# Moving a runtime branch and a small projection ahead of the last product of a mixture of experts

## The chip, the cores and the metric

The kernel runs on one core of one Trainium2 chip. The time is device microseconds of one execution; lower is better. In the profile, PE is TensorE's matmul stream, PEld its weight loads, DVE VectorE, ACT ScalarE, POOL GpSimd and SP SyncE, which issues every DMA of this kernel. A small q behind an engine's name (SPq, PEldq) means its instruction queue: branches, register loads, semaphore instructions and DMA issues.

## The reference, cut to what matters

Two layers of a decoder trunk over 256 tokens of width 1024, all float32. Each layer has a token mixer, a norm, a channel mixer, a second norm, and a per-layer embedding. The channel mixer of layer 0 is dense; the one of layer 1 is the mixture of experts that the change is about. Only the end of layer 1 is touched:

```python
def moe_swiglu(x, w_router, w1, w3, w2):      # x: 256 x 1024, 8 experts, d_ff 3584
    top_logits, top_e = lax.top_k(x @ w_router, 2)
    gates = softmax(top_logits)
    # for each expert e, over the tokens that chose it:
    y = (silu(x_e @ w1[e]) * (x_e @ w3[e])) @ w2[e]
    # each token adds its two experts' y, each times its gate

h = layer_norm(ALPHA * h + moe_swiglu(h, ...), g, b)
h = h + sigmoid(h @ ple_gate) * (p @ ple_proj)   # p: 256 x 256
```

## The kernel before, in words

**Words and buffers.** Weights ("words") come in loads of mostly 1 MB through one function, `load_raw` (line 79). It takes the next buffer of a cycle over the rings that are open at that point: raw (4 buffers of 1 MB), side (3), post (3) and early (2), in the mixture twelve in all. SP issues the loads in the order of the program, and each waits for its buffer to be free. `split_unit` (line 94) splits words into a high part (ACT, line 103) and a low part (DVE, line 111); `mm3` (lines 142 to 144) multiplies with three matmuls.

**The mixture** (`swiglu_moe`, line 987). Experts are ranked by how many tokens chose them. Ranks 0 to 4 have room for 128 tokens (class `Big`, split words), rank 5 for 64 and ranks 6 and 7 for 32 (class `Small`, words used unsplit, 128/n row groups of the array side by side). `STEPS` is the order, written out by hand: 26 pairs (rank, column block). Each step runs in `experts_in` (line 1312): the up product with w1, SiLU, the down product of the step before, the up product with w3, `sl` = `sl` times gate times that product (line 1367), and, after an expert's last block, `put_back`. `gather` (line 1096) makes a one-hot matrix `oh` from token slots, multiplies the tokens out with it, transposes them, and also transposes `oh` itself into `ohT` (line 1138) and takes each row's gate as `gs` (lines 1140 and 1144). `put_back` (lines 1202 and 1288) splits the down product, multiplies by `ohT`, and `add_back` (line 1303) adds into `h` with a running row sum for the norm. The last step is (6, 1): rank 6, the second block of 1536 of its 3584 columns, whose down product needs six loads of 1 MB.

**The end.** After step (6, 1): its `turn` (line 1253, PE transposes and an ACT copy), its down product (line 1283), then `closing` (line 1412), which is called ahead of the put-back: it loads p, transposes it (line 280), loads and splits the words of ple_proj and the first 1 MB of ple_gate (the latter's low part on POOL), and loads the two rows of the norm (line 347). Then the put-back. Then a flag is read into a register on every engine (`values_load`, line 1385) and `tc.If` (line 1386) branches past a further round of all experts, which is needed only where an expert got more tokens than it has places; for these inputs it is skipped. A block of `If` is scheduled as a unit: nothing behind it runs ahead of it. Its round takes words through the raw ring alone, since `closing` has taken the others out. Then, outside, `norm_turn` (line 403) runs with `ple_project` (line 326, 24 matmuls over 4 banks, then 4 ACT copies) between its parts on PE, and `ple` (line 433) with 96 matmuls of the gate, sigmoid, product, sum, and the output's DMAs.

```python
                before_[0].down(gT, before_[1])
                rest = closing() if base == 0 else None
                finish_last()
...
            flag = nc.values_load(over[0:1, 0:1], min_val=0, max_val=1)
            with tc.If(flag > 0):
                experts(1)
```

Of the kernel before, what the change touches and what calls it, by code (L numbers as in the profile page):

```python
# [28 lines left out]
PLE = 256  # L29
# [24 lines left out]
def body(ctx, tc, nc, I, out):  # L54
# [115 lines left out]
    slots = consts.tile([128, 256], FT, name="slots")  # L170
# [12 lines left out]
    def fill_constants(words):  # L183
        left = [0]

        def scratch(shape, dt):
# [3 lines left out]
            if len(shape) == 2:  # L190
# [16 lines left out]
        nc.gpsimd.iota(slots, pattern=[[1, 256]], base=1, channel_multiplier=0,  # L207
                       allow_small_or_imprecise_dtypes=True)
        nc.vector.memset(halfpi, PI / 2)
# [193 lines left out]
    def norm_turn(hT, produce, gb, sm, z, sq, each=None, meanwhile=None):  # L403
# [3 lines left out]
        if produce is None:  # L407
            bring = meanwhile()
# [8 lines left out]
        if produce is not None:  # L417
            bring = meanwhile and meanwhile()
# [568 lines left out]
    def swiglu_moe(hT, logits, closing):  # L987
        hh, hl = hT
        with tc.tile_pool(name="moe", bufs=1, reuse_waits="tile") as mp:
# [11 lines left out]
            lg2 = mp.tile([128, NT, 2, N_EXP], FT, name="lg2")  # L1001
            nc.vector.tensor_copy(lg2, ps)
            lg = mp.tile([128, NT, N_EXP], FT, name="lg")
# [9 lines left out]
            ohe = mp.tile([128, NT, 2, N_EXP], FT, name="ohe")  # L1013
# [20 lines left out]
            xg_h = pers.tile([128, KD, 256], FR, name="xgh", tag="hTh")  # L1034
            xg_l = pers.tile([128, KD, 256], FR, name="xgl", tag="hTl")
# [19 lines left out]
            def ranks():  # L1055
# [12 lines left out]
                words = mp.tile([128, 1024], FT, name="words", tag="sl")  # L1068
# [27 lines left out]
            def gather(r, n, off, half):  # L1096


                small = n < 128
                sr, gr = (slot, gate) if r == 0 else (slot_r, gate_r)  # L1100
                oh = mp.tile([128, NT, 128], FR, name="oh", tag="oh", bufs=1)
                for t in range(NT):
                    done["oh"] = nc.vector.tensor_scalar(
                        oh[:, t].rearrange("p (j s) -> p j s", s=n),
                        slots[:, None, off:off + n].to_broadcast([128, 128 // n, n]),
                        sr[:, t, r:r + 1], None, op0=OP.is_equal)
# [5 lines left out]
                for f in range(2):  # L1112
                    fs = slice(f * 512, (f + 1) * 512)
                    p = work()
                    for t in range(NT):
                        nc.tensor.matmul(p, oh[:, t], hsh[:, t, fs], start=t == 0, stop=False)
                        nc.tensor.matmul(p, oh[:, t], hsl[:, t, fs], start=False, stop=t == NT - 1)
                    nc.scalar.activation(xs[:, fs], p, AF.Copy)
                if small:
                    x = mp.tile([128, KD, 64], FT, name="xe", tag="xe", bufs=1)[:, :, :n]  # L1120
                    p = work()[:, :KD * n].rearrange("p (a b) -> p a b", b=n)
                    for k in range(KD):
                        nc.tensor.transpose(p[:, k], xs[:n, k * 128:(k + 1) * 128], ident[:n, :n])
                    nc.scalar.activation(x, p, AF.Copy)
                else:
                    b0 = half * 128
                    x = xg_h[:, :, b0:b0 + 128], xg_l[:, :, b0:b0 + 128]
                    for k0 in range(0, KD, 4):
                        p = work().rearrange("p (a b) -> p a b", a=4)
                        for j in range(4):  # L1130
                            nc.tensor.transpose(p[:, j], xs[:, (k0 + j) * 128:(k0 + j + 1) * 128], ident)
                        ins = split_sb(x[0][:, k0:k0 + 4], x[1][:, k0:k0 + 4], p)
                    if off == 0 and r == 0:
                        table("silu_and_others", ins)
# [12 lines left out]
            class Big:  # L1147
# [4 lines left out]
                def __init__(self, r, got):  # L1152
                    self.r, (self.x, self.ohT, self.gs) = r, got
                    self.y = None

# [38 lines left out]
                def y_split(self, w, ys):  # L1194
                    yh = mp.tile([128, D], FR, name="yh", tag="gh")
                    yl = mp.tile([128, D], FR, name="yl", tag="gl")
                    for f, y in enumerate(ys):
                        fs = slice(f * w, (f + 1) * w)
                        split_sb(yh[:, fs], yl[:, fs], y)
                    return yh, yl  # L1200

                def put_back(self):
                    yh, yl = self.y_split(512, self.y)
                    for f in range(2):
                        fs = slice(f * 512, (f + 1) * 512)
                        for t in range(NT):
                            p = work()
                            nc.tensor.matmul(p, self.ohT[:, t], yh[:, fs], start=True, stop=False)
# [3 lines left out]
            class Small(Big):  # L1212
# [44 lines left out]
                def down(self, gT, c):  # L1257
                    if self.y is None:
                        self.y = acc()[:, :D // self.q]
# [219 lines left out]
```

## Time and profile before

| | us |
|---|---|
| median of 3 runs | 1515.63 (1511.83 to 1517.67) |
| the profiled execution | 1511.99 |
| its span, first to last instruction | 1510.2 |
| PE busy, share of the span | 1421.4, 94% |
| DVE busy | 975.8, 65% |
| ACT busy | 812.8, 54% |

The profile numbers everything in microseconds from the start of the span. A busy share counts overlapping work of an engine once, so PE at 94% says that PE is hardly ever empty, not that it is at its peak. The DMA share is the mean over the core's 16 DMA engines. Idle time of an engine costs something only where a later stage waits for it, so each stretch has to be asked which resource it waits for last. The mixture runs from about 598 to 1471 us; what is behind it is the norm, the projection and the gate.

### The profile page before, as it was taken

What the parts mean: (1) busy time and instruction counts of PE and PEld (TensorE: products, weight loads), DVE (VectorE), ACT (ScalarE), POOL (GpSimd) and SP (SyncE); (2) the same over time, 40 slices, a digit from 0 to 9 for tenths busy, and PEclk for the clock granted to TensorE, in tenths of its full rate; (3) what the DMA queues carried; (4) which work ended last, traced back from release to release, by engine and by line L of the source; (5) the groups of instructions that cost most, each with busy time, mean ns of one, the idle gap of its engine ahead of it and who ended that gap; (6) DMA issues with size and microseconds to landing.
All of it is one profiled execution on the core that took longest, in us unless ns stands there. A gap on an engine that the chain in (4) does not pass through costs nothing. (4 is left out here: it accounts for less than half of the span.)

```text
span 1510.2 us, 19841 instructions
## 1 busy us (share of the span) xinstructions
PE 1421.4 (94%) x7298; PEld 1054.7 (70%) x7298; DVE 975.8 (65%) x1347; ACT 812.8 (54%) x1120; POOL 8.1 (1%) x16
## 2 busy tenths in 40 slices
PE   7999899999999997988999989999899997999968
PEld 6677788888786776746877668853478755777736
DVE  7676654554676767626888568930288854898745
ACT  5466543443555466526766457720277644777534
POOL 0000000000000000000000000000000000000000
PEclk9999999999999998999999999999999999999989
DMA  8643655454346642999999999999999999999893
GB/s 282 221 153 133 223 185 205 167 192 171 99 150 206 224 154 75 383 419 412 406 413 344 408 405 413 416 382 398 414 407 413 405 408 412 407 413 403 304 362 112
DMA packets 125065, 456.84 MB, mean 303 GB/s; under 512 B 10976, under 2 KB 22048, under 8 KB 103200
## 3 DMA queue, kind: packets, MB, share of 16 engines
q1 hardware_dynamic: 124960, 455.50, 78.2%
q8 instruction: 59, 0.97, 0.3%
q14 instruction: 46, 0.38, 0.1%
HBM read 454.42 MB, written 1.05 MB: 302 GB/s over the span
## 5 line engine op out<-in xcount | busy, mean ns | idle before, releaser
L111 DVE TENSOR_TENSOR wlo<-raw,whi 128x1024 fp32r<-128x1024 f32 (+1 forms) x238 | 282.0, 1214 | 91.4 <-ACT whi L103 86.7
L103 ACT ACTIVATE whi<-raw 128x1024 fp32r<-128x1024 f32 (+1 forms) x238 | 243.1, 1052 | 119.9 <-PE acc L143 54.6
L142 PE MATMUL wk<-whi,xgh 128*128 128x512 f32 x560 | 224.0, 400 | 14.9 <-ACT whi L103 14.9
L143 PE MATMUL wk<-whi,xgl 128*128 128x512 f32 x560 | 221.4, 395 | 0.0
L111 DVE TENSOR_TENSOR wlo<-post,whi 128x1024 fp32r<-128x1024 f32 x132 | 157.6, 1219 | 74.2 <-ACT whi L103 72.4
L144 PE MATMUL wk<-wlo,xgh 128*128 128x512 f32 x560 | 201.8, 399 | 3.0 <-DVE wlo L111 3.0
L103 ACT ACTIVATE whi<-post 128x1024 fp32r<-128x1024 f32 x132 | 135.7, 1056 | 110.8 <-DMA post<-in_moe_w_dram 63.2
L111 DVE TENSOR_TENSOR wlo<-side,whi 128x1024 fp32r<-128x1024 f32 x136 | 162.2, 1218 | 15.5 <-ACT whi L103 9.9
L142 PE MATMUL acc<-whi,gh 128*128 128x512 f32 x392 | 155.1, 396 | 8.9 <-ACT whi L103 7.9
L143 PE MATMUL acc<-whi,gl 128*128 128x512 f32 x392 | 154.3, 394 | 0.0
L103 ACT ACTIVATE whi<-side 128x1024 fp32r<-128x1024 f32 x136 | 139.8, 1056 | 25.7 <-PE acc L143 14.2
L144 PE MATMUL acc<-wlo,gh 128*128 128x512 f32 x392 | 142.8, 395 | 0.5
L142 PEld LDWEIGHTS wk<-whi,xgh 128*128 128x128 f32 x560 | 106.9, 191 | 43.6 <-ACT whi L103 19.9
L144 PEld LDWEIGHTS wk<-wlo,xgh 128*128 128x128 f32 x560 | 105.2, 191 | 29.3 <-DVE wlo L111 7.2
L143 PEld LDWEIGHTS wk<-whi,xgl 128*128 128x128 f32 x560 | 106.9, 191 | 22.3 <-DVE xgl L138 0.2
L1367 DVE SCALAR_TENSOR_TENSOR sl<-sl,gs,wk 128x512 f32<-128x512 f32 (+2 forms) x43 | 30.2, 732 | 140.7 <-PE wk L1240 94.0
L142 PEld LDWEIGHTS acc<-whi,gh 128*128 128x128 f32 x392 | 73.5, 188 | 31.5 <-ACT whi L103 12.8
L142 PE MATMUL wk<-whi,hTh 128*128 128x512 f32 x224 | 88.7, 396 | 2.7 <-ACT whi L103 2.7
L144 PE MATMUL wk<-wlo,hTh 128*128 128x512 f32 x224 | 87.9, 393 | 0.0
L143 PE MATMUL wk<-whi,hTl 128*128 128x512 f32 x224 | 87.8, 392 | 0.0
L144 PEld LDWEIGHTS acc<-wlo,gh 128*128 128x128 f32 x392 | 72.7, 188 | 20.9 <-DVE wlo L111 4.4
L143 PEld LDWEIGHTS acc<-whi,gl 128*128 128x128 f32 x392 | 73.6, 188 | 16.6
(396 smaller groups left out, 2119.4 us busy)
## 6 DMA issues: line engine op xcount, KB each, us to landing
raw<-in_moe_w_dram SPq DMA_DIRECT2D x96, 1024.0 KB, 15.2
side<-in_moe_w_dram SPq DMA_DIRECT2D x75, 1024.0 KB, 15.1
post<-in_moe_w_dram SPq DMA_DIRECT2D x75, 1024.0 KB, 15.6
early<-in_moe_w_dram SPq DMA_DIRECT2D x50, 1024.0 KB, 15.8
raw<-in_ffn_w_dram SPq DMA_DIRECT2D x19, 1024.0 KB, 5.2
raw<-in_w_in_dram SPq DMA_DIRECT2D x15, 1024.0 KB, 7.3
post<-in_ffn_w_dram SPq DMA_DIRECT2D x14, 1024.0 KB, 5.2
raw<-in_moe_w_dram SPq DMA_DIRECT2D x17, 768.0 KB, 6.6
```

What stands on the lines that cost most here:

```text
L103: nc.scalar.activation(hi, v, AF.Copy)
L111: engine.tensor_sub(lo, v, hi.bitcast(FT))
L142: nc.tensor.matmul(ps, xh, wh, start=first, stop=False)
L143: nc.tensor.matmul(ps, xl, wh, start=False, stop=False)
L144: return nc.tensor.matmul(ps, xh, wl, start=False, stop=last)
L1367: nc.vector.scalar_tensor_tensor(sl[:, fs], sl[:, fs], now.gs, p, op0=OP.mult, op1=OP.mult)
```

## The change

Five edits.

1. The down product and put-back of step (6, 1) leave `experts_in`, which now returns after the step's `turn`. Behind it come, in this order: the rings but raw are taken away, the branch, the rings are given back, p is loaded and turned and the projection is done and copied out, the down product, the loads of the norm's rows, the put-back.
2. The flag is read at the fourth step of the mixture, not at the branch.
3. Rank 6 is accumulated and put back one block at a time (`by_step`), so there is a put-back of (6, 0) in the middle of the mixture, in the step behind it.
4. `gather` no longer transposes `oh` and no longer takes gates; `put_back` makes `ohT` itself (`back_of`): a diagonal of the slots (DVE), a matmul with a matrix of -1 (PE), a comparison (DVE). The gate is applied by `add_back` instead of by the product with w3.
5. The put-back of a small expert takes the row groups innermost, four banks at once. The early split of the gate's first words (ACT, POOL) goes. Code for other sizes of small experts comes in, and is not used with the sizes here.

```diff
+            def back_of(r, off, w, blocks):
+                sr = slot if r == 0 else slot_r
+                dg = mp.tile([128, NT, 128], FT, name="dg", tag="oh", bufs=1)
+                p = work()[:, :256]
                 for t in range(NT):
...
+                    nc.vector.tensor_scalar(dg[:, t], ident, sr[:, t, r:r + 1], None, op0=OP.mult)
+                    nc.tensor.matmul(p[:, t * 128:(t + 1) * 128], negones, dg[:, t], start=t == 0, stop=t == NT - 1,
+                                     skip_group_check=True)
+                ohT = []
+                for j in range(blocks):
+                    ohT.append(mp.tile([128, NT, 128], FR, name="ohT", tag="ohT", bufs=3))
+                    nc.vector.tensor_scalar(ohT[j], p.rearrange("p (t b) -> p t b", t=NT), float(off + j * w),
+                                            numbers[:, 128 // w // 2:128 // w // 2 + 1], op0=OP.add, op1=OP.is_equal)
+                return ohT
...
-                p = work()
-                ohT = mp.tile([128, NT, 128], FR, name="ohT", tag="ohT", bufs=3)
-                for t in range(NT):
-                    nc.tensor.transpose(p[:, t * 128:(t + 1) * 128], oh[:, t].bitcast(FT), ident)
-                for t in range(NT):
-                    nc.tensor.matmul(p[:, 256:257], oh[:, t].bitcast(FT), gr[:, t, r:r + 1],
-                                     start=t == 0, stop=t == NT - 1)
-                nc.scalar.activation(ohT, p[:, :256].rearrange("p (t b) -> p t b", t=NT), AF.Copy)
-                gs = mp.tile([128, 1], FT, name="gs", tag="gs", bufs=3)
-                nc.vector.tensor_copy(gs, p[:, 256:257])
-                return x, ohT, gs
...
                 def put_back(self):
+                    ohT = back_of(self.r, self.off, self.n, self.m)
+                    yh, yl = self.y_split(512, self.y)
...
-            def add_back(t, f, w, p):
+            def add_back(r, t, f, w, p):
                 fs = slice(f * w, (f + 1) * w)
-                nc.vector.scalar_tensor_tensor(h[:, t, fs], h[:, t, fs], 1.0, p, op0=OP.mult, op1=OP.add,
+                nc.vector.scalar_tensor_tensor(h[:, t, fs], p, (gate if r == 0 else gate_r)[:, t, r:r + 1], h[:, t, fs],
+                                               op0=OP.mult, op1=OP.add,
                                                accum_out=(sums if w == 512 else quarters)[:, t, f:f + 1])
...
                 def finish_last():
                     ex, c = before_
-                    if c == len(ex.cols) - 1:
+                    if c == len(ex.cols) - 1 or (base == 0 and ex.r == seq[-1][0]):
                         ex.put_back()
 
                 for s, (r, c) in enumerate(seq):
                     now = made[r]
+                    if s == 3 and base == 0:
+                        flag.append(nc.values_load(over[0:1, 0:1], min_val=0, max_val=1))
+                    if base == 0 and r == seq[-1][0] and c == 0:
+                        now.by_step(c)
...
-                turn_last()
-                before_[0].down(gT, before_[1])
-                rest = closing() if base == 0 else None
-                finish_last()
-                if rest is not None:
-                    rest()
-
-            experts(0)
-
-            flag = nc.values_load(over[0:1, 0:1], min_val=0, max_val=1)
-            with tc.If(flag > 0):
+                if base:
+                    turn_last()
+                    before_[0].down(gT, before_[1])
+                    finish_last()
+                    return
+                ex, c = before_
+                n = ex.cols[c][1] // 128
+                gT = mp.tile([128, 4, 128], FT, name="gk", tag="xe", bufs=1)[:, :n // 4]
+                return ex, c, ex.turn(g, c, gT)
+
+            flag = []
+            ex, c, gT = experts(0)
+
+            own = closing[0]()
+            with tc.If(flag[0] > 0):
                 experts(1)
+            closing[1](own)
+            ex.by_step(c)
+            ex.down(gT, c)
+            closing[2]()
+            ex.put_back()
             return sums
...
+                def away():
+                    return {n: rings.pop(n) for n in ("early", "post", "side")}
+
+                def project(own):
+                    rings.update(own)
                     n = PLE // 128 * S
...
+                    words = chunk("side")
+                    parts = [words[:, j * n:(j + 1) * n].rearrange("p (k s) -> p k s", s=S).bitcast(FR)
+                             for j in range(2)]
+                    ple_turn(i, pool.tile([128, NT, PLE], FT, name="pt", tag="sg", bufs=1), *parts)
+                    kept["pp"] = chunk("early").rearrange("p (t d) -> p t d", t=NT)
+                    ple_project(ple_weights(i), *parts, kept["pp"])()
+                    del rings["early"]
+
+                def vectors():
+                    kept["gb"] = load_gb("ffn", i, halves(chunk("post")))
+
+                closing = away, project, vectors
```

## Rows read from the trace of the kernel before

**Rows 1.** The page, 40 slices of the span: GB/s that the DMA engines moved.

```profile
GB/s 282 221 153 133 223 185 205 167 192 171 99 150 206 224 154 75 383 419 412 406 413 344 408 405 413 416 382 398 414 407 413 405 408 412 407 413 403 304 362 112
```

**Rows 2.** A stretch of 10 us (columns: PE, PEld, DVE, ACT, POOL busy; PE's clock; DMA share; GB/s).

```profile
1400.00:1410.00 10.00, 9.45 (x44) 7.46 (x43) 5.83 (x6) 4.82 (x7) 0.00 (x0) 1.00 0.64 256
```

**Rows 3.** Timeline: last w3 load, a slab read, turn's copy, down product, last load before the branch.

```profile
1434.95 0.42 SPq L87 DMA_DIRECT2D side<-in_moe_w_dram  x1
...
1447.86 0.83 PE L1240 MATMUL wk<-side,xe 128*32 128x384 f32 x8
...
1452.66 0.49 ACT L1254 ACTIVATE ge<-wk 128x384 f32<-128x384 f32 x1 [7.88 <-PE wk L1253]
...
1458.04 0.79 SPq L347 DMA_DIRECT2D post<-in_ln_ffn_b_dram  x1
1458.61 1.07 PE L1283 MATMUL acc<-post,ge 128*32 128x256 f32 x16 [1.42 <-DMA post<-in_moe_w_dram]
...
1461.19 0.64 PE L1283 MATMUL acc<-early,ge 128*32 128x256 f32 x8 [0.66 <-DMA early<-in_moe_w_dram]
```

**Rows 4.** DMA issues, us to landing: that w3 load, that last load, gate words alone.

```profile
side<-in_moe_w_dram SPq DMA_DIRECT2D x1, 768.0 KB, 11.1
...
post<-in_ln_ffn_b_dram SPq DMA_DIRECT2D x1, 512.0 KB, 13.2
...
raw<-in_ple_gate_dram SPq DMA_DIRECT2D x3, 1024.0 KB, 5.1
```

**Rows 5.** Line 1386, the branch (columns: duration in ns min/median/max; first and last start).

```profile
L1386 SPq EVENT_SEMAPHORE  x8: 17/17/17, 1465.0 to 1471.3; - x8
...
L1386 PEldq COMPARE_BRANCH  x1: 5782/5782/5782, 1464.2 to 1464.2; - x1
...
L1386 DVEq COMPARE_BRANCH  x1: 72/72/72, 1469.7 to 1469.7; - x1
...
L1386 DVEq EVENT_SEMAPHORE  x1: 21/21/21, 1472.7 to 1472.7; - x1
```

**Rows 6.** Waits of SP's queue (us in total, times, longest): the first load behind the branch.

```profile
SPq L87 <- DVEq L1386: 1.3, 1, 1.3
```

**Rows 7.** Timeline of the put-back and the norm: split, first add, last matmul, sums, tile 0.

```profile
1461.96 0.38 ACT L137 ACTIVATE yh<-acc 128x256 fp32r<-128x256 f32 x1 [8.80 <-PE acc L1283]
...
1463.50 0.42 DVE L1305 SCALAR_TENSOR_TENSOR h<-h,wk 128x256 f32<-128x256 f32 x1
1463.85 0.08 DVE L1305 DVE_READ_ACCUMULATOR h<-h,wk 128x1 f32 x1
...
1464.09 0.27 PE L1297 MATMUL wk<-yl,ohT 32*128 32x256 f32 x1
...
1469.02 2.34 DVE L1301 TENSOR_TENSOR sums<-quarters 128x4 f32<-128x4 f32 x1
...
1472.77 0.21 DVE L386 TENSOR_SCALAR lnnm<-sums 128x1 f32<-128x1 f32 x1 [1.41 <-DVEq L1386]
...
1476.28 1.41 DVE L400 SCALAR_TENSOR_TENSOR h<-raw,lnrs,post 128x512 f32<-128x512 f32 x2
```

**Rows 8.** The chain that ended last (start, us, what): projection, turn, gate, sigmoid.

```profile
1472.82 0.76 PE acc L142
...
1476.14 0.43 PE acc L143
...
1481.17 1.75 PE wk L280 x16
1482.92 0.23 PE acc L142
...
1505.11 0.61 ACT sg L440
```

**Rows 9.** A stretch of 1 us within the projection (columns as in rows 2).

```profile
1477.00:1478.00 1.00, 1.00 (x3) 0.79 (x3) 0.96 (x4) 0.60 (x1) 0.00 (x0) 0.50 1.04 401
```

**Rows 10.** Timeline of rank 0's gather: the matmuls that take the gates.

```profile
598.41 0.50 PE L1140 MATMUL wk<-gate,oh 128*128 128x1 f32 x4
```

More of the change, by code (lines that the diff above doesn't have):

```diff
@@ L1094, in of_expert, with gather @@
                 return I[name][0, bass.ds(expert[r], 1)].rearrange("e k n -> (e k) n")
[L1096 to L1101, printed above, removed]
+            def back_of(r, off, w, blocks):
+                sr = slot if r == 0 else slot_r
+                dg = mp.tile([128, NT, 128], FT, name="dg", tag="oh", bufs=1)
+                p = work()[:, :256]
                 for t in range(NT):
[L1103 to L1106, printed above, removed]
+                    nc.vector.tensor_scalar(dg[:, t], ident, sr[:, t, r:r + 1], None, op0=OP.mult)
[7 more added lines that the diff above has]
+                return ohT
+            def gather(r, n, off, x):
+                sr = slot if r == 0 else slot_r
+                oh = mp.tile([128, NT, 128], FR, name="oh", tag="oh", bufs=1)[:, :, :n]
+                for t in range(NT):
+                    done["oh"] = nc.vector.tensor_scalar(oh[:, t], slots[:, :n], float(off), sr[:, t, r:r + 1],
+                                                         op0=OP.add, op1=OP.is_equal)
                 if off == 0 and r == 0:
@@ L1226, in rows, with pieces, block @@
+                def pieces(self, w):
+                    for j in range(self.m):
+                        o = 0
+                        while o < w:
+                            at = j * w + o
+                            n = min(512 - at % 512, w - o)
+                            yield j, o, at // 512, at % 512, n
+                            o += n
                 def rows(self, u):
                     return slice(u * self.n, (u + 1) * self.n)
+                def block(self, j):
+                    return slice(j * self.n, (j + 1) * self.n)
@@ L1235, in up @@
                         if between is not None and k == 4:
                             between()
[L1237 removed]
+                        for j, o, b, at, wd in self.pieces(w):
                             for u in range(self.q):
[L1239 to L1241 removed]
@@ L1242, in up @@
-                    return ps
-                def turn(self, g, c):
-                    w = self.cols[c][1] // self.q
-                    gT = mp.tile([128, 8, 128], FT, name="ge", tag="gh")
-                    for j0 in range(0, w // 128, 4):
-                        m = min(4, w // 128 - j0)
+                                nc.tensor.matmul(ps[b][self.rows(u), at:at + wd], self.x[:, k, self.block(j)],
+                                                 raw[:, k % m, u * w + o:u * w + o + wd],
+                                                 start=k == 0 and at == 0, stop=k == KD - 1, skip_group_check=True)
@@ L1282, in multiply @@
+                            for i in range(2):
+                                self.multiply(gT, raw[:, i], w // 128 - 1, u - 1 + i, w)
+                def multiply(self, gT, raw, i, u, w):
+                    first = self.left == self.whole
+                    self.left -= 1
+                    for j, o, b, at, wd in self.pieces(self.w):
                         for f in range(self.q):
-                            nc.tensor.matmul(self.y[self.rows(f)], gT[:, j, self.rows(u)],
-                                             raw[:, f * w:(f + 1) * w], start=self.left == D_FF // 128 - 1,
+                            nc.tensor.matmul(self.y[b][self.rows(f), at:at + wd],
+                                             gT[:, j * (w // 128) + i, self.rows(u)],
+                                             raw[:, f * self.w + o:f * self.w + o + wd], start=first and at == 0,
```

226 lines of the change are left out of this document (112 added, 114 removed).

## The prediction

> **What bounds the kernel now.** I read the page's slices first, to see which resource is full where, then the stretches in which it is not, then the last 70 us instruction by instruction, because all that the change reorders lies there. From the 17th slice on, DMA moves some 400 to 420 GB/s [rows 1]: the mixture is a stream of words, and PE, though 94% busy, mostly waits with it. A load of 1 MB takes 1.049 MB / 412 GB/s = 2.55 us of that stream. Towards the end PE falls behind for once: from 1400 to 1410 us it is busy throughout and DMA only at 0.64 [rows 2]. All twelve buffers are full there, so work added on PE a little earlier counts one for one, and work added elsewhere in the mixture doesn't.
>
> The words of the last down product reach PE as they land; it ends at 1461.19 + 0.64 = 1461.8 us [rows 3]. From there to the end, 48 us, little streams and the rest is a chain: put-back, branch, projection and norm, turn, gate, output. So a part of that chain that moves in front of 1461.8 is a gain only as far as the words are not made later.
>
> **The branch.** SP's eight semaphore instructions at the branch run from 1465.0 to 1471.3 us [rows 5]; the last of its loads was issued at 1458.04 and landed 13.2 us later, at 1471.2 [rows 3, 4]. So SP passes when what it issued has landed, and need not wait for the engines. The engines pay differently: PE's branch lasts 5.8 us, DVE's 0.07 us, but its next instruction comes 3.0 us behind it [rows 5]. And a load into a buffer of the raw ring, which the skipped round uses too, waited until DVE was past the branch: 1.3 us [rows 6].
>
> [...]
>
> **The change, part by part (profiled execution, 1511.99 us).**
>
> *Words later.* The last w3 load lands at 1434.95 + 11.1 = 1446.05 us [rows 3, 4]. Before, six loads were queued behind it by then; now SP issues nothing until that moment, and the queue runs dry. Next in the program is p (256 KB, issued at once), then the load of ple_proj. Counting the loads of the trace round the cycle of twelve buffers puts it into a side buffer, and with one of the three taken for the turned p, the next one free is that of the slab read from 1447.86 on, some 0.65 us [rows 3]: issue at 1448.5. Alone on the queue 1 MB takes 5.1 us [rows 4]: landed at 1453.6. Six loads at 2.55 us follow, up to 1468.9 us. The third goes to raw, so it waits for ACT and DVE. These are done with the turn at 1452.66 + 0.49 = 1453.15 [rows 3], and past the branch 3.0 to 5.8 us later. At 5.8 the last four loads land by 1459.0 + 5.1 + 3 x 2.55 = 1471.7. So the words land between 1468.9 and 1471.7.
>
> *PE before the last product.* PE leaves the turn at 1452.6 and the branch at 1455.6 to 1458.4; I take 5.8 us, PE's own row. Turning p and its first copy take about 1.5 us, an estimate from 16 transposes in 1.75 us [rows 8], doubled for the clock, and a copy of 0.38 [rows 7]: 1459.9. [...] The new branch leaves PE idle for as long, so I take 8.35 again: 1468.3. Then six loads at 1.07 us [rows 3], 6.4: the product ends at 1474.7, later than its words. That is 12.9 us later than before. Bounds: 1470.0 (1.1 behind the first value for the words) and 1480.5 (the first rival).
>
> *Put-back.* Before, 1461.8 to the end of the sums at 1471.4: 9.5 us, in which the splits of the projection's words stood between the adds and POOL's next to the last sum, which took 2.34 us for 4 columns [rows 7]. Without them: first add 1.54 behind the split's start, eight adds 0.35 apart, 0.3 for the sum, and up to 0.5 because the four banks now end together: 5.0. Its new matrices need no product, so they are made while PE waits: 0, or 1 us on this path if they are not. Gain 4.5.
>
> *Branch off the end.* 1471.4 to 1472.77: gain 1.4 [rows 7].
>
> *Norm to gate.* Before, from 1472.77 to the gate's first matmul at 1482.9, 10.1 us, with PE on the projection until 1481.2 [rows 7, 8]. The norm of tile 0 was done 1476.28 + 1.41 - 1472.77 = 4.9 us behind its start [rows 7], and turn and split take half of 1.75, 0.9: 5.8. Gain 4.3, bounds 3.5 and 5.4.
>
> *Clock at the gate.* Before, the projection had brought the clock back when the gate began. Now PE stands for some 7 us ahead of the turn. If it comes back as slowly as in rows 8 and 9, about 4.5 us of the gate run at 0.43 for 0.23: 10 matmuls x 0.2 = 2.1 us lost, bounds 0 and 2.6. The gate's words are no longer split ahead; ACT and DVE are idle enough behind the product to hide it, and without that cover a copy and a subtraction, some 2.7 by columns from rows 3 and 7, come on top.
>
> *In the mixture.* The extra put-back of (6, 0) falls some 130 us ahead of the stretch of rows 2, where PE is already behind: its 16 matmuls took 1462.34 to 1464.36, 2.0 us [rows 7]. I take 2.0; bounds 0 (absorbed) and 4.0 (its adds also delay the splits on DVE). For a large expert the gather loses two transposes and two gate matmuls and the put-back gains two matmuls: 0. Rank 0's gate matmuls, 0.50 [rows 10], leave PE's path at the start of the mixture: -0.5. The early read of the flag, the product with w3 without the gate and the new constants at the start stand beside full queues or change no pass: 0, or 1.5 for seven DVE instructions of 0.21 [rows 7] if nothing hides the constants.
>
> **Sum:** 12.9 - 4.5 - 1.4 - 4.3 + 2.1 + 2.0 - 0.5 = +6.3 us on 1511.99. The median of the runs shown is 3.6 above that execution, so against it 1515.63 + 6.3 = 1521.9, 0.4% slower. Half a percent, 7.6 us, is about what a measurement of this kernel can tell from no change.
>
> **Rivals.**
>
> *The words wait for the engines (slower).* If the first load behind the branch, not only one into raw, waits as that of rows 6 did, ple_proj goes out at 1459.0 and not at 1448.5, the six loads land by 1459.0 + 5.1 + 15.3 = 1479.4, and the product ends at 1480.5: 5.8 more than the forecast, 1527.7. For it speaks that row; against it that side, post and early are not used by the skipped round. It decides from an issue at 1453.3 on; before that PE's 1474.7 ends last.
>
> *The branch is cheap (about even).* If the engines pass in 3 us or less, the projection starts when its words have landed and been split, 1453.6 + 2.7 = 1456.3, and ends at 1464.7, hidden by the stream. Then the words bound at 1470.0, 4.7 less, and a shorter idle time may keep the clock: 2.1 less. That leaves -0.5, with the extra put-back absorbed -2.5: 1513 to 1515. [...]
>
> *PE keeps up (faster).* If the lighter gathers let PE follow the stream before 1410, the idle 36% of those 10 us, 3.6 us, comes back as well; with the cheap branch that gives -6 to -8, 1508 to 1510. Against it: a large expert's PE work is the same by the count above.
>
> That the projection isn't ahead, because PE takes the first words of the product before it, would change little: the work on PE in front of 1474.7 is the same.
>
> **How the numbers follow.** Forecast 0.50 (its own range 1515 to 1528, by the bounds above), words late 0.25, cheap branch 0.17, PE keeps up 0.08. Slower by over 0.5%, beyond 1523.2: most of the second case and a third of the forecast, 0.39. Faster, below 1508: 0.11. Within: 0.50. The range 1508 to 1532 takes in the words-late case with its extra put-back at 4, and the cheap branch, and leaves out a fifth.
>
> **What would show it.** Right: no load is issued between the last w3 load and about 1446; DMA runs dry for some 5 us there; PE's branch lasts over 3 us with the clock at 0.5 behind it; the projection stands in front of the last down product; that product ends 10 to 15 us later than before; put-back, norm and turn follow without a gap, and the gate's first matmuls run at 0.43. Wrong: a product that ends before 1468 or behind 1480; a gate at full clock from its start; or a mixture whose last w3 load lands more than 4 us off 1446.

## Result, and the profile after

The changed kernel took 1533.53 us (median of four runs, 1531.85 to 1535.02), the kernel before 1515.88 in the same comparison: ratio 1.012 (95%: 1.0096 to 1.0144), 18 us slower. The forecast was 1521.9 with a range up to 1532, so the time lies 1.5 us outside it, on the side to which the forecast leaned.

**Where the time went.** I cut both traces at one place, the issue of the last w3 load of step (6, 1): what lies between the first load of the mixture's words into the early ring and it is called the mixture here, what lies behind it the end. Before: 568.73 to 1434.95, 866.2 us, and 75.3 us to the end of the span [rows 3]. After: 567.24 to 1446.12, 878.9 us, and 84.4. So by these two profiles the mixture lost 12.7 us and the end 9.1. (The runs below show that the profiled execution of before had a short mixture; the lasting loss is 6 to 7.)

*The mixture.* PE's waits in it, from 600 to 1470 us (what waited, for whom: us in total, times, longest):

```profile
PE wk L1338 <- DVE ohT L1114: 5.6, 3, 2.3
...
PE wk L142 <- DVE h L1351: 4.0, 3, 2.4
PE wk L1216 <- DVE ohT L1114: 3.6, 4, 1.8
```

L1338 and L1216 are the put-back matmuls of a small and of a large expert, seven put-backs with 9.2 us of waits for the comparison. PE stands at the put-back until DVE has compared, and DVE has splits of words (L111, 1.22 us each) ahead of the comparison. The put-back of (6, 0), on DVE and then on PE:

```profile
1284.21 1.22 DVE L111 TENSOR_TENSOR wlo<-post,whi 128x1024 fp32r<-128x1024 f32 x1
1285.34 1.28 DVE L138 TENSOR_TENSOR xg<-wk,xg 128x512 fp32r<-128x512 f32 x2
1286.54 0.47 DVE L1114 TENSOR_SCALAR ohT<-wk,numbers 128x256 fp32r<-128x256 f32 x1
```

```profile
1284.13 0.61 PE L1109 MATMUL wk<-dg,negones 128*128 128x128 f32 x4
1287.07 0.40 PE L1338 MATMUL wk<-yh,ohT 32*128 32x256 f32 x4 [2.32 <-DVE ohT L1114]
...
1290.23 0.77 PE L142 MATMUL wk<-whi,xg 128*128 128x512 f32 x1 [2.42 <-DVE h L1351]
```

The diagonal's matmul is done at 1284.74; the comparison of 0.47 us runs only at 1286.54, behind splits that DVE began at 1284.21 and that take it 2.3 us. Then the next product waits for the adds that hold the four banks.

*The end.* SP's issues (they answer to rows 3) and DMA's busy share in 1 us slices from 1440 to 1480 (answers to rows 2):

```profile
1446.12 0.33 SPq L87 DMA_DIRECT2D side<-in_moe_w_dram  x1
1446.50 0.45 SPq L332 DMA_DIRECT2D pt<-in_p_dram  x1
1459.25 0.34 SPq L87 DMA_DIRECT2D post<-in_moe_w_dram  x1
1461.46 0.39 SPq L87 DMA_DIRECT2D side<-in_ple_proj_dram  x1
...
1470.81 0.86 SPq L1312 DMA_DIRECT2D raw<-in_moe_w_dram  x2
```

```profile
DMA  8998999999999998200078999999500479999999
```

The queue is dry twice: from 1456 to 1460, while SP is held at the branch, and from 1468 to 1472, while the raw loads wait for DVE to be past it. The loads did not go out in the order of the text: p's went ahead of the branch (1446.50, SP's branch at 1447.0), so the section on the kernel is too strict where it says that nothing behind a block of `If` runs ahead of it. SP's last semaphore instruction at the branch comes at 1458.6, where the last w3 load had landed at 1457.5 and p at 1458.2. The branch (answers to rows 5; durations in ns):

```profile
L1442 SPq EVENT_SEMAPHORE  x8: 17/17/17, 1455.3 to 1458.6; - x8
...
L1442 DVEq COMPARE_BRANCH  x1: 76/76/76, 1464.7 to 1464.7; - x1
L1442 PEldq COMPARE_BRANCH  x1: 5972/5972/5972, 1465.3 to 1465.3; - x1
...
L1442 DVEq EVENT_SEMAPHORE  x1: 21/21/21, 1470.4 to 1470.4; - x1
```

PE behind it (answers to rows 8): turn of the last step, branch, p's turn, projection with 0.43 us from one matmul to the next until 1479.85 (0.63 in the records, which overlap), last product.

```profile
1464.66 0.61 PE L1292 MATMUL wk<-ident,sl 128*128 128x128 f32 x3 [0.68 <-DVE sl L1271]
1471.65 1.08 PE L290 MATMUL wk<-ident,pt 128*128 128x128 f32 x4 [6.37 <-PEq L1442]
...
1474.15 0.80 PE L142 MATMUL acc<-whi,side 128*128 128x512 f32 x1 [0.56 <-ACT whi L103]
...
1482.83 1.07 PE L1321 MATMUL acc<-post,gk 128*32 128x256 f32 x16
...
1499.48 3.68 PE L290 MATMUL wk<-ident,h 128*128 128x128 f32 x16 [9.62 <-DVE h L410]
1502.81 0.78 PE L142 MATMUL acc<-whi,hGh 128*128 128x512 f32 x1
```

The product ends at 1488.2, the sums at 1493.40 (5.2 us later, answers to rows 7); from there DVE's queue holds the turn back. Two z, two splits of gate words and only then tile 0's reciprocal:

```profile
1493.44 0.21 DVE L396 TENSOR_SCALAR lnnm<-sums 128x1 f32<-128x1 f32 x1
1493.69 1.28 DVE L401 SCALAR_TENSOR_TENSOR post<-h,lnnm,post 128x1024 f32<-128x1024 f32 x1
...
1495.02 1.22 DVE L111 TENSOR_TENSOR wlo<-raw,whi 128x1024 fp32r<-128x1024 f32 x1
1496.15 1.28 DVE L401 SCALAR_TENSOR_TENSOR post<-h,lnnm,post 128x1024 f32<-128x1024 f32 x1
1497.35 1.22 DVE L111 TENSOR_TENSOR wlo<-raw,whi 128x1024 fp32r<-128x1024 f32 x1
1498.48 0.16 DVE L404 RECIPROCAL lnrs<-lnss 128x1 f32<-128x1 f32 x1
```

### The profile page after: what moved, and what is told of

Its sections match the earlier page's. It is cut to its first block, busy times and chain, and to the rows that moved or that the text cites. A ratio compares the mean times of both kernels' runs of the same rounds, so it can differ in the third digit from the quotient of the medians.

```text
span 1530.5 us, 19899 instructions
## 1 busy us (share of the span) xinstructions
PE 1423.5 (93%) x7302; PEld 1058.7 (69%) x7302; DVE 988.3 (65%) x1393; ACT 816.0 (53%) x1116; POOL 3.6 (0%) x15
## 3 DMA queue, kind: packets, MB, share of 16 engines
q1 hardware_dynamic: 124960, 455.50, 77.7%
## 5 line engine op out<-in xcount | busy, mean ns | idle before, releaser
L111 DVE TENSOR_TENSOR wlo<-raw,whi 128x1024 fp32r<-128x1024 f32 (+1 forms) x236 | 280.4, 1214 | 88.9 <-ACT whi L103 83.2
L142 PE MATMUL wk<-whi,xg 128*128 128x512 f32 x560 | 225.7, 404 | 17.5 <-ACT whi L103 13.5
L143 PE MATMUL wk<-whi,xg 128*128 128x512 f32 x560 | 223.2, 399 | 0.0
L144 PE MATMUL wk<-wlo,xg 128*128 128x512 f32 x560 | 208.6, 401 | 2.3 <-DVE wlo L111 2.3
L111 DVE TENSOR_TENSOR wlo<-post,whi 128x1024 fp32r<-128x1024 f32 x134 | 160.0, 1219 | 49.4 <-ACT whi L103 47.1
L111 DVE TENSOR_TENSOR wlo<-side,whi 128x1024 fp32r<-128x1024 f32 x140 | 167.5, 1220 | 15.4 <-ACT whi L103 9.4
L103 ACT ACTIVATE whi<-side 128x1024 fp32r<-128x1024 f32 x140 | 144.8, 1057 | 31.2 <-PE acc L143 15.7
L142 PEld LDWEIGHTS wk<-whi,xg 128*128 128x128 f32 x560 | 108.2, 193 | 48.1 <-ACT whi L103 20.1
L144 PEld LDWEIGHTS wk<-wlo,xg 128*128 128x128 f32 x560 | 106.5, 193 | 28.9 <-DVE wlo L111 6.2
L143 PEld LDWEIGHTS wk<-whi,xg 128*128 128x128 f32 x560 | 108.3, 193 | 22.2 <-DVE xg L138 0.4
L111 DVE TENSOR_TENSOR wlo<-early,whi 128x1024 fp32r<-128x1024 f32 x66 | 78.5, 1218 | 3.6 <-ACT whi L103 2.8
```

The lines of the kernel that those rows point to most:

```text
L103: nc.scalar.activation(hi, v, AF.Copy)
L111: engine.tensor_sub(lo, v, hi.bitcast(FT))
L142: nc.tensor.matmul(ps, xh, wh, start=first, stop=False)
L143: nc.tensor.matmul(ps, xl, wh, start=False, stop=False)
L144: return nc.tensor.matmul(ps, xh, wl, start=False, stop=last)
```

## Experiments

All results first. "Mixture" runs from the first load into the early ring to the last w3 load, "product" from the last w3 load to the end of the last down product, "end" from the last w3 load to the end of the span, so it includes the product; all three are from the one profiled execution. Ratios are to the kernel before, run on the same chip, where its median was 1514.3 to 1515.9 us; compare kernels by them, and not by their medians.

| kernel | median us | ratio (95%) | mixture | product | end |
|---|---|---|---|---|---|
| before | 1515.88 | 1 | 866.2 | 26.9 | 75.3 |
| after | 1533.53 | 1.0120 (1.0096 to 1.0144) | 878.9 | 42.1 | 84.4 |
| early_matrices | 1530.39 | 1.0088 (1.0059 to 1.0118) | 877.0 | 40.9 | 83.1 |
| old_end | 1518.40 | 1.0029 (1.0012 to 1.0047) | 871.0 | 27.1 | 76.6 |
| before_two_put_backs | 1516.33 | 1.0007 (0.9991 to 1.0022) | 873.5 | 27.0 | 74.2 |
| bank_by_bank | 1533.17 | 1.0102 (1.0064 to 1.0139) | 879.7 | 41.8 | 83.6 |
| one_put_back | 1531.38 | 1.0109 (1.0091 to 1.0127) | 875.8 | 42.2 | 84.9 |
| branch_last | 1527.42 | 1.0075 (1.0056 to 1.0095) | 879.1 | 34.8 | 79.2 |
| project_beside | 1535.78 | 1.0147 (1.0120 to 1.0174) | 877.2 | 42.3 | 86.4 |
| norm_first | 1532.65 | 1.0115 (1.0096 to 1.0134) | 879.8 | 41.9 | 85.5 |
| after_no_branch | 1521.46 | 1.0045 (1.0028 to 1.0063) | 880.1 | 34.7 | 75.6 |
| before_no_branch | 1514.71 | 0.9997 (0.9984 to 1.0011) | 871.4 | 27.6 | 73.9 |
| mixture_undone | 1524.81 | 1.0071 (1.0050 to 1.0092) | 872.1 | 41.5 | 84.1 |
| before_project_first | 1518.32 | 1.0028 (1.0018 to 1.0037) | 874.3 | 27.3 | 77.7 |
| words_ahead | 1537.21 | 1.0132 (1.0096 to 1.0168) | 878.0 | 48.9 | 89.8 |
| words_ahead_mix_undone | 1530.96 | 1.0095 (1.0066 to 1.0124) | 871.9 | 49.5 | 90.6 |
| all_ahead | 1529.26 | 1.0087 (1.0060 to 1.0115) | 879.7 | 39.3 | 82.7 |
| all_ahead_mix_undone | 1523.35 | 1.0045 (1.0028 to 1.0063) | 868.9 | 39.1 | 83.8 |

Read the mixture column first: the old mixture has 866.2, 871.4 and 874.3, the changed one 877.2 to 880.1 in eight executions with whatever end. A difference of less than some 4 us in this column says little by itself.

### The mixture

**early_matrices.** The matrices of all ranks but 6 are made behind their gather:

```diff
+ if base == 0 and r != seq[-1][0]:
+     made[r].ohT = back_of(r, off, made[r].n if n < 128 else 128, 1)
  ...
- ohT, = back_of(self.r, self.off, 128, 1)
+ ohT, = self.ohT or back_of(self.r, self.off, 128, 1)
```

> The changed kernel, but the put-back matrices of ranks 0 to 5 and 7 are made right behind their gather (same comparison, kept until the put-back, as the kernel before kept its transposed ones); only rank 6 still compares at its two put-backs. Theory 1 (PE waits in order for a comparison that stands behind weight splits in DVE's queue, at every put-back of the mixture, and that is most of the 11 us by which the last w3 load is late): the waits for ohT at the large put-backs go, the last w3 load goes out at 1436 to 1440 instead of 1446, and the time is 1523 to 1527 us. Rival 2 (the lag is the second put-back of rank 6 and the four banks of a small put-back, not the comparison): at most 2 us better, 1531 to 1534.

The large put-backs' waits for ohT are gone, and of the small ones' 5.6 us 0.6 stay. The time falls by 0.0032 of 1515 us, some 5 us (the two intervals overlap), and the last w3 load comes 2 us earlier: less than theory 1, more than rival 2. So the comparison is a part; (6, 0), untouched here, keeps its own waits:

```profile
PE wk L1109 <- DVE dg L1108: 2.5, 1, 2.5
...
PE wk L142 <- DVE h L1351: 2.2, 2, 1.9
```

**old_end.** The changed kernel with the old order from the last step on (one put-back of rank 6, branch last, projection beside the norm, gate words split ahead).

> The changed kernel with the whole end of the kernel before: one put-back of rank 6, branch behind it, projection beside the norm, gate words split ahead. The mixture keeps its comparisons at the put-back and its gates in the add. Theory 1: the lag of the mixture stays but for the one comparison of (6, 0): 6 to 10 us slower than before, 1522 to 1526. Rival 2: without the second put-back of rank 6 little lag is left: 1516 to 1519. Whatever it is, its distance to 1533.5 is what the new end and the second put-back cost together.

1518.4: 2 to 7 us slower than before by the interval, in rival 2's range, with a mixture of 871.0 us, as the old one has. So the comparisons at the put-backs, with a single put-back of rank 6, cost some 4 us. The new end and the second put-back are worth the other 14.

**before_two_put_backs.** In the kernel before:

```diff
- if c == len(ex.cols) - 1:
+ if c == len(ex.cols) - 1 or (base == 0 and ex.r == seq[-1][0]):
      ex.put_back()
```

> The kernel before with one part of the change alone: rank 6 is put back after each of its two steps, with the transposed matrix that its gather made. Theory 1: 16 matmuls and eight adds more, 0 to 3 us: 1516 to 1519, last w3 load at 1435 to 1438. Rival 2: the second put-back alone makes most of the lag: 1521 to 1527, last w3 load behind 1440.

The second put-back alone, its matrix ready, costs 1 us (-1.4 to +3.3). Rival 2 is out in this form. The w3 load is later than in theory 1's expectation (1441.10), but so it is in before_no_branch (1440.89): before's profiled mixture was a short one.

**bank_by_bank.** The loop over f around the matmuls of a small put-back again, one bank at a time.

> The changed kernel, but a small put-back writes one bank after the other, as before, instead of four banks together. Theory 1: the banks are not what PE waits for; within 2 us of 1533.5. Rival 2: PE's next product no longer waits for four adds (2.4 us at each of four small put-backs of which the trace shows the one of (6, 0)); 3 to 6 us better, 1527 to 1530, with the last w3 load at 1440 to 1443.

Same time within the interval: no loss by the banks shows.

**one_put_back.** The product of (6, 0) waits in SBUF (the edit in short):

```diff
- ex.put_back()                        # of (6, 0)
+ nc.scalar.activation(self.y0, self.y[0], AF.Copy)
  ...
+ nc.vector.tensor_add(self.y0, self.y0, self.y[0])   # ahead of the last y_split
```

> The changed kernel without the put-back of (6, 0) in the mixture: the product of that step is copied out of its bank (256 columns on ACT) and added to the last step's product ahead of the one put-back at the end (about 0.4 us on DVE there). Theory 1 (the put-back of (6, 0) with its comparison costs what the load issues show, 7.5 to 8 us between the 280th and the 305th load): last w3 load at 1438 to 1440, time 1525 to 1528 us. Rival 2 (as the kernel before with two put-backs had it against its runs, ratio 1.0007, it costs 1 us or so): 1531 to 1533.5.

The mixture is 3 us shorter, the last w3 load at 1442.68. The time falls by about 2 us, into the rival's range; the intervals overlap.

**mixture_undone.** early_matrices and one_put_back together.

> The changed kernel with both edits of the mixture undone: matrices of ranks 0 to 5 and 7 made at the gather, one put-back of rank 6 (its first product kept in SBUF). If the two add up (2 to 3 us and 2 to 4 us), the last w3 load is 871 to 874 us behind the first instead of 879, and the time 1525 to 1528 us: what is left over before is then the tail alone, 9 to 10 us. If they stand for the same wait, 875 to 877 and 1529 to 1531.

They add up: 872.1 us, as the old mixture, and 0.0049 of 1515, 7 us, come back (3 to 12 by the two intervals). On PE nothing waits for ohT any more, and for the adds 0.3 us. The end is as long as in the changed kernel, 84.1. The pairs below with and without this edit give 6 us twice more (0.0037 and 0.0042). So the mixture lost 6 to 7 us, by the comparison at the put-back and by the put-back of (6, 0) with one. The gates in the add stay in this run and cost nothing that shows.

### The end

**branch_last.** The branch behind the last put-back, the projection still ahead of the last product (without the lines that take the rings away and give them back):

```diff
- with tc.If(flag[0] > 0):
-     experts(1)
  closing[1](own)
  ...
  ex.put_back()
+ with tc.If(flag[0] > 0):
+     experts(1)
```

> The changed kernel with the branch behind the last put-back again, the projection still ahead of the last product. Theory 1 (it is the branch in its new place that makes the tail long: PE stands 6.0 us, SP issues no words from 1446.5 to 1459.3, and the raw loads wait for DVE): the last product ends 8 to 10 us nearer to the last w3 load (42 us behind it in the changed kernel), the branch costs 3 to 4 us behind the sums, and the time is 1525 to 1530 us. Rival 2 (it is the projection's 8.6 us on PE, and the branch only moves): the product ends 5 to 6 us nearer and the branch costs as much at the end: 1532 to 1536.

Mostly theory 1: the product ends 7 us nearer, between the two theories; DVE pays 3.5 us at the old place; the time falls by 7, as theory 1 said. Against after_no_branch the branch still costs 0.0030 here, some 4.5 us. DVE there:

```profile
1490.48 0.21 DVE L396 TENSOR_SCALAR lnnm<-sums 128x1 f32<-128x1 f32 x1 [3.53 <-DVEq L1448]
```

**project_beside.** Branch ahead, projection beside the norm again.

> The changed kernel with the branch ahead of the last product, but the projection (splits and matmuls) beside the norm again; p is turned where it was. Theory 1 (branch): the product is then bound by its words, of which the last landed at 1484 in the changed kernel, so it ends 3 to 5 us nearer to the last w3 load, and 1 to 3 us come back between norm and gate: 1530 to 1533 us. Rival 2 (projection): the product ends 8 us nearer, norm to gate takes 10 instead of 9.4: 1525 to 1527.

Both are out: by the ratios it is 4 us slower than the changed kernel, with overlapping intervals. The product, without the projection in front, ends no earlier, since its words came late: its first load behind the branch goes into raw and went out at 1467.25, when ACT was past the branch (1467.21). With the branch there, nothing is won by taking the projection out from ahead of the product.

**after_no_branch.** Branch, flag and further round left out.

> The changed kernel with the branch, the read of its flag and the further round left out (with these inputs the round is skipped anyway). Theory 1 (the branch in its new place costs about 5 us more than behind the put-back, where it cost 3.5): the last product ends 33 to 35 us behind the last w3 load instead of 42, 1523 to 1526 us. Rival 2 (PE's stop at the branch only fills a wait for words): at most 3 us, 1530 to 1533.

11 us come back by the ratios (1.0120 to 1.0045; 7 to 16 by the two intervals), 8.8 by the two profiles' ends: more than theory 1 said. The early read of the flag is gone too, but the mixture, 880.1, is no shorter. PE goes from turn to turn, and the product is bound by its words:

```profile
1464.35 0.61 PE L1292 MATMUL wk<-ident,sl 128*128 128x128 f32 x3 [0.68 <-DVE sl L1271]
1464.80 0.60 PE L290 MATMUL wk<-ident,pt 128*128 128x128 f32 x4
...
1480.25 0.64 PE L1321 MATMUL acc<-raw,gk 128*32 128x256 f32 x8 [0.64 <-DMA raw<-in_moe_w_dram]
```

**before_no_branch.** The same left out of the kernel before.

> The kernel before with branch, flag and further round left out. It prices the branch at the end. If it costs what DVE shows (1.4 us from the sums to the norm), 1513 to 1515 us; if it costs what PE shows (idle for 8.4 us ahead of the projection, which holds the turn), 1507 to 1511. It is also a second execution of the old mixture: the last w3 load 866 us behind the first load as in the one profile, or 868 to 871 if that execution was a short one.

Ratio 0.9997: at the end the branch cost between nothing and 2.4 us; the 1.4 us that DVE shows are within that, the 8.4 of PE are not. The stretches from 1475 to 1487 show why PE's are not (length, then PE, PEld, DVE, ACT, POOL busy, granted clock, DMA share, GB/s):

```profile
1475.00:1478.00 3.00, 3.00 (x14) 2.44 (x13) 2.90 (x5) 2.59 (x4) 3.00 (x2) 0.99 0.47 165
1478.00:1481.00 3.00, 1.10 (x5) 0.56 (x4) 2.96 (x3) 1.25 (x4) 1.51 (x1) 1.00 0.51 199
1481.00:1484.00 3.00, 1.04 (x5) 1.04 (x6) 2.93 (x6) 1.78 (x4) 0.00 (x0) 0.65 0.91 341
1484.00:1487.00 3.00, 3.00 (x15) 2.59 (x13) 2.29 (x4) 2.63 (x6) 0.00 (x0) 0.50 0.24 24
```

In the kernel before:

```profile
1475.00:1478.00 3.00, 3.00 (x8) 2.30 (x7) 2.93 (x6) 2.02 (x4) 0.00 (x0) 0.50 1.04 403
1478.00:1481.00 3.00, 3.00 (x13) 2.34 (x12) 1.22 (x2) 2.37 (x3) 0.00 (x0) 0.93 0.81 262
1481.00:1484.00 3.00, 3.00 (x22) 2.63 (x21) 1.68 (x3) 2.91 (x7) 0.00 (x0) 1.00 0.88 337
```

There PE stood at the branch, ran the projection at a granted clock of 0.50 until 1478, and came to the gate, at 1482.92, at 1.00 [rows 8, 9]. Without the branch the projection is over by 1479.1, PE stands ahead of the turn instead, and the gate begins at 0.50.

**before_project_first.** In the kernel before, the projection's matmuls between put-back and branch.

> The kernel before with one step moved: the projection's 24 matmuls run between the put-back and the branch (all else of the end as it was). [...] If PE only reaches the branch later by the projection and everything behind moves with it, 1515 to 1520.

4 us slower. PE reaches the branch later, then stands for 7.5 us until the norm of tile 0 is there, and runs turn and first gate matmuls at 0.50 (1487 to 1493). In the kernel before, PE ran the projection beside the norm, and the granted clock was 1.00 at the gate.

**norm_first.** Tile 1's norm and the splits of the first four gate units are ordered behind tile 0 (the edit in short):

```diff
- n0.finish()
+ fi = n0.finish()
  turn_tile(h, KD, *hT, 0)
- ahead[:] = [AHEAD, last["lo"]]
+ ahead[:] = [0, last["lo"]]; zi = fi
```

> The changed kernel, but DVE finishes and splits the norm of tile 0 before tile 1's norm and before the splits of the gate's first words. If DVE's order is why the norm took 9.4 us to the gate's first matmul instead of the 5.8 forecast, that becomes 6 to 7 us and the time 1529.5 to 1531.5 us. If the gate then waits for its own words' splits, nothing is won: 1532.5 to 1534.5.

The gate's first matmul comes 5.5 us behind the norm's start instead of 9.4, and nothing is won: the granted clock was still 0.50 until 1504. Part of the 5.5 is only an order: tile 1's turn now stands inside the gate. Turn and gate together show it better: they begin 2.4 us earlier behind the norm's start (3.7 instead of 6.0) and take 29.6 us instead of 25.9. Of these 3.7 us, 1.8 are a wait for the split of a gate word; most of the rest goes with the granted clock, 0.50 until 1504 and 0.65 from there to 1507 (columns as above; the last row is of the changed kernel, where its gate begins):

```profile
1498.00:1501.00 3.00, 2.30 (x7) 1.06 (x5) 2.26 (x5) 2.92 (x6) 0.00 (x0) 0.50 0.00 0
1501.00:1504.00 3.00, 1.75 (x5) 1.36 (x6) 3.00 (x5) 2.76 (x3) 0.00 (x0) 0.50 0.00 0
1504.00:1507.00 3.00, 3.00 (x14) 2.65 (x13) 1.65 (x3) 1.20 (x2) 0.00 (x0) 0.65 0.00 0
```

```profile
1502.00:1505.00 3.00, 3.00 (x13) 2.62 (x12) 3.00 (x5) 2.95 (x5) 0.00 (x0) 0.68 0.00 0
```

**words_ahead.** ple_proj and the six loads of the last product issued ahead of the branch, in buffers that the further round does not use.

> The changed kernel, but the load of ple_proj and the six loads of the last down product are issued ahead of the branch, into the eight buffers that the further round does not use, so that SP waits at the branch with words in flight. Theory 1a (the branch costs by the dry queue: SP issued nothing from 1446.5 to 1459.3 and the raw loads waited for DVE until 1470.8): the last product ends 36 to 38 us behind the last w3 load instead of 42, 1526 to 1529 us. Theory 1b (it costs by PE's own order: branch 6.0, p's turn 2.5, projection 8.6 with the clock at half, product 5.4, with all words there): the product ends where it did, within 1.5 us, 1531 to 1534 us.

Neither: the load of p fell behind the branch, where SP stood until the last of its loads had landed. Its events end at 1477.3, and PE waited:

```profile
1480.22 1.08 PE L290 MATMUL wk<-ident,pt 128*128 128x128 f32 x4 [15.88 <-DMA pt<-in_p_dram]
```

**words_ahead_mix_undone.** The same with mixture_undone.

> The same loads ahead of the branch, and both mixture edits undone as in mixture_undone: the nearest to a version of this change that is worth keeping. Theory 1a: 1517 to 1521 us, about the kernel before. Theory 1b: 1523 to 1526, as mixture_undone.

Slower than either theory, for the same wait for p; only the difference to words_ahead counts.

**all_ahead.** p's load too ahead of the branch.

> As words_ahead, but the load of p too goes out ahead of the branch: in words_ahead it had fallen behind it and went out at 1477.3, when SP's last load had landed, and PE waited 15.9 us for it. So only now no load that PE needs stands behind the branch. Theory 1a (dry queue): the last product ends 34 to 38 us behind the last w3 load, 1525 to 1529 us. Theory 1b (PE's own order): the product ends 39 to 42 us behind it, 1530 to 1534 us.

No load that PE needs before the last product ends is behind the branch, and yet it ends 39.3 us behind the last w3 load, in 1b's range, where without a branch it was 34.7. PE:

```profile
1463.45 0.61 PE L1292 MATMUL wk<-ident,sl 128*128 128x128 f32 x3 [0.68 <-DVE sl L1271]
1470.82 1.09 PE L290 MATMUL wk<-ident,pt 128*128 128x128 f32 x4 [6.75 <-PEq L1457]
...
1487.31 0.39 PE L1351 MATMUL wk<-yh,ohT 32*128 32x256 f32 x4 [2.67 <-DVE ohT L1114]
```

So of the 7.4 us (42.1 to 34.7), 4.6 stay with the words there, which leaves PE's own stop, 6.75 us, and the matmuls behind it, 0.44 us apart up to 1474.3. The other 2.8 are at most the dry queue: 1.9 of them lie in the projection, which took 6.8 us to the product's first matmul instead of 8.7, as its matmuls came 0.23 us apart again 3.5 us behind the start of p's turn, and in the changed kernel only 8.5 us behind it; no run shows why. The time, 1529.3, lies between the two ranges; the interval doesn't separate them. The last line is the theory of the mixture once more, at the end: a gate split now stands ahead of the comparison, and the last put-back waits 2.7 us for it.

**all_ahead_mix_undone.** The best that I found of this change.

> all_ahead with both mixture edits undone. Theory 1a: 1518 to 1522 us. Theory 1b: 1523 to 1527 us, slower than the kernel before by what PE's stop and the half clock behind it cost.

As 1b: 1523.4, still 0.45% slower than the kernel before.

## Why the prediction missed

It forecast +6.3 us and got 18. By its steps:

- **In the mixture (the step that failed most).** "Its new matrices need no product, so they are made while PE waits: 0, or 1 us" and "For a large expert the gather loses two transposes and two gate matmuls and the put-back gains two matmuls: 0". I counted instructions and not whom they wait for. The matrix came from PE and ACT, steps ahead of its use; now DVE, PE and DVE again hand it over to PE at the moment of use, behind whatever DVE has queued. I had +1.5 for the mixture; the runs show 6 to 7 (mixture_undone), of which the bare second put-back is about 1 (I took 2.0) and the comparisons with one put-back about 4 (old_end).
- **Words later, PE before the last product.** Right in mechanism: SP held until its loads landed, the queue dry, the raw loads waiting for DVE, PE's branch 6.0 us (5.8 taken), the projection 8.7 (8.35 taken, the 1472.82 to 1481.17 of rows 8), at a granted clock of 0.50 until about 1480. That the clock would be as low as in rows 9 was my estimate: PE had stood for 8.5 us ahead of those, and here it stood for 6.4 with 0.59 granted during its branch. The product ends 42.1 us behind the last w3 load, 39.8 were forecast: p's turn took 2.5 instead of 1.5, and the branch began at 1465.3, 7.8 us behind the landing of the last w3 load at 1457.5, where I had taken the turn 6.6 behind it. PE set the end, as forecast: the last product waits for no load.
- **Put-back and branch off the end.** The put-back took 5.2 us where I had 5.0 (its 0.3 for the sum and 0.5 for the banks were my estimates; the sum took 0.16), and the norm starts right behind the sums, as forecast.
- **Norm to gate, and the clock.** 9.4 us instead of 5.8, but the clock's price, which I had booked in the gate, is part of it. The turn begins 6.0 us behind the norm's start where I had 4.9, because the gate's splits and tile 1 came between on DVE. Then both tiles are turned at half clock ahead of the gate's first matmul: 3.3 us to it, where the kernel before took 1.7 and I had 0.9 for one tile. Turn and gate together take 25.9 us here and 24.1 before, so by this difference the clock cost 1.8, near the 2.1 forecast, and the turn and the gate's first matmul ran at 0.50 (1499.48 to 1503). Norm to the gate's end is 31.9 here, 32.3 before and 33.3 in norm_first. I had added up as independent two terms that trade against each other.
- **The rivals.** "The branch is cheap" is out: the same branch costs 11 us here. In the old place of the kernel before it costs at most 2.4 us, so before_no_branch neither confirms nor refutes the 1.4 that I booked as a gain. DVE's own branch instruction took 0.076 us, but its next one comes 5.7 us behind it, and PE's own took 5.97. "The words wait for the engines" didn't happen in that form: ple_proj went out at 1461.46, ahead of DVE's 1470.4 (in project_beside, where the first load goes into raw, it did). "PE keeps up" had it the wrong way round.

By the two profiles the end grew by 9.1 us where +4.8 was forecast: 15.2 for the product, less 4.3 for the put-back, 1.4 for the branch and 0.4 from the norm to the gate's end. With the mixture's 5 us over the forecast, that is most of the miss; the rest is within the intervals. By removal, the two causes make up the whole: 6 to 7 us of mixture and 11 of branch for the 18 measured. That both removed together bring the kernel back to the time before was not run.

Left open: why the old mixture varies from 866 to 874 us between executions, what share of the mixture's loss is the comparison at (6, 0) alone, and how much of the branch's 11 us is the dry queue.

## What to carry to other kernels

An operand that is made just before its use costs its place in the queue of every engine that takes part, not its instructions: here comparisons of 0.47 us cost PE 9.2 us of waits in seven put-backs, as splits stood ahead of them, and the time about 4 us. The branch here held the issuing queue until its loads had landed and stopped each engine for 2.5 to 6.7 us, so put it where the stream has ended anyway and where the granted clock is up again before the next long product, as in the kernel before (0.50 behind the branch, 1.00 at the gate): there it cost at most 2.4 us, with the projection moved ahead of it some 4.5 (branch_last), in the stream 11. When you shorten a stretch in which TensorE idles ahead of a long product, look at the granted clock at the product's start before you book the gain: it was 0.50 at the gate in before_no_branch and before_project_first, and nothing was won.

## What the runs showed of the hardware that I had not expected

In these runs the length of the branch's stop went with the words in flight, and not with its place. Between its two dry spells, from 1460 to 1468, the queue of the changed kernel was full again, and DVE came to the branch at 1464.68: a DMA share of 0.69 over its 5.75 us. In project_beside the branch stands at the same place, the first load behind it went out only at 1467.25, and the stop is 2.95 us on DVE and 3.4 on PE. The stretch of DVE's stop in both (columns as above; changed kernel first):

```profile
1464.68:1470.43 5.75, 0.60 (x3) 0.36 (x3) 0.00 (x0) 0.49 (x1) 0.00 (x0) 0.65 0.69 279
```

```profile
1463.45:1466.40 2.95, 0.59 (x3) 0.36 (x3) 0.00 (x0) 0.49 (x1) 0.00 (x0) 1.00 0.04 11
```

The other runs agree: every stop of PE, DVE or ACT with a DMA share of 0.49 or more lasted 4.6 to 6.7 us, every one with 0.15 or less 2.5 to 4.0. One lies between: 3.8 on PE in branch_last at 0.37. In words_ahead DVE's took 5.6 at a share of 1.03. In the kernel before, PE's 5.8 us [rows 5] fell into a share of 0.69 and DVE's 3.0 into one of 0.07 (ACT's 2.8: 0.12; in the changed kernel PE's 6.0: 0.56, ACT's 5.0: 0.57), so the two prices between which I had to choose were one branch at two loads of the queue. Why an engine stops there, and why for longer beside words in flight, no run here shows.

DVE's instructions beside POOL's split took longer by more than I had read from one row. In before_no_branch, tile 0's z took 3.13 us with POOL at its split, and 1.28 for tile 1 right after it:

```profile
1477.47 3.13 DVE L391 SCALAR_TENSOR_TENSOR raw<-h,lnnm,post 128x1024 f32<-128x1024 f32 x1
...
1480.76 1.28 DVE L391 SCALAR_TENSOR_TENSOR raw<-h,lnnm,post 128x1024 f32<-128x1024 f32 x1
```

The sum of 4 columns took 1.91 us there and 0.16 in the changed kernel, which has no POOL work beside it. Both ended with POOL: its two splits end at 1477.16 and 1479.51, the sum at 1477.18 and tile 0's z at 1480.60, 1.1 us behind the second, about what it takes alone.
